# A down projection in groups of two column blocks, some pairs of k-tiles by seven products instead of eight, and a thin gate's weights in one piece

## The chip, the cores and the metric

The kernel runs on one core of one Trainium2 chip. The metric is the device time of one execution in microseconds (us). The engines are called PE (TensorE; PEld is its weight load), DVE (VectorE), ACT (ScalarE), POOL (GpSimd) and SP (SyncE, which here issues the weight loads).

## The reference, cut to what matters

Two blocks are applied to a sequence of 256 tokens of width 2048, all in fp32. The change touches the end of the second block, its gated feed-forward layer, and the very first product of the first block.

```python
# first block: 48 narrow columns of proj (ml_i, ml_f, dn_b, dn_a) are the "thin gate"
u = _rmsnorm(h, norm_w)
proj = jnp.matmul(u, w_in)
...
# second block, FFN_HIDDEN = 5632
h = rmsnorm(x, ffn_norm_w[l])
x = x + (jax.nn.silu(h @ w_gate[l]) * (h @ w_up[l])) @ w_down[l]
return rmsnorm(x, final_norm_w)
```

## The kernel before, in words

**fp32 products from three passes.** Each operand is cut into a high part (cast to fp32r on ACT) and the rest (a subtraction on DVE). A product of two k-tiles is then three matmuls: high by high, high by rest, rest by high. For weights this is `cut`: one ACT cast (L312) and one DVE subtraction (L314) for each piece of 1024 columns, that is two k-tiles of 512. The 256 tokens are two tiles of 128; a normal piece is 12 matmuls of 128x512 (2 k-tiles, 2 token tiles, 3 passes).

**The stream.** All weights are one list of pieces. `run_stream` goes through it: it loads five pieces ahead (SP, tag `wr`, 5 buffers), cuts up to three pieces ahead (tags `wh`, `wl`, 5 buffers each), issues the piece's matmuls, and after each piece lets every side generator go one step (`advance`). What follows a product (evacuation, activation, transposes, the making of the next operand) is such a generator. The order written in the program is a priority: a scheduler at build time orders each engine's queue by it, taking what is ready.

**Seven products instead of eight.** `Pair` computes two 512-column blocks X and Y together. For a pair of k-tiles, two token tiles and two blocks there are eight products of 128x128 by 128x512. For the pairs in `SPAIRS` (1, 3, 5 of 8) it uses Strassen's scheme in Winograd's form: seven products, in four pieces A, E, B, C, whose weights are sums made on DVE (`cut`, L305 to L308, four ops of 128x512), and whose operand forms s1 to s4 are sums of the operand's tiles. The other pairs are two plain pieces X and Y. A sum of products is kept in a PSUM bank of its own: four from the pool `pm` (tag `mm`) and, from the first A on, three from the pool `ps` (tag `sp`). Each pool has four banks, and transposes take theirs from `ps` (`bank`). Before, only the gate and up projections of the feed-forward layer use `Pair`.

**The feed-forward stage.** The hidden width is 11 blocks of 512, in three parts `PARTS` of 4, 4 and 3. For each part, each block is one `Pair` of w_gate and w_up columns (8 pairs of k-tiles; `ff_mid` after the last C, `ff_done` at the end: it evacuates, applies the gate, transposes the block's hidden values on PE (L237) and cuts them into the operand `opf`). Then the part's down projection follows: four chunks of 512 columns n = 0..3, each with 16 k-tiles (12 in the last part) by plain products, with two `pm` banks; `ff_down` adds each to the residual `hw[n]`, scaled by `sc3`. After the last part the final norm is made and written out.

**The start.** `startup` issues the four loads of x and the loads of the first four pieces. The first seven pieces are the thin gate's weights, of 1, 1, 2, 3, 3, 3, 3 k-tiles (`FIRST`), each loaded from two column ranges (32 and 16 columns). Then x is transposed chunk by chunk and turned into the operand (`operand`: an ACT and a DVE op for each of 16 k-tiles, written to `hl`), and `stats` squares x for the norm (ACT, eight ops with a sum).

Of the kernel before, what the change touches and what calls it, by code (L numbers as in the profile page):

```python
# [11 lines left out]
F32 = mybir.dt.float32  # L12
# [7 lines left out]
P = 128  # L20
D = 2048
S = 256
# [11 lines left out]
AHEAD = 5  # L34
SPAIRS = (1, 3, 5)
PARTS = ((0, 4), (4, 8), (8, 11))
WN = 1024
WU = 14
STEP = 2
FIRST = [1, 1, 2, 3, 3, 3, 3]  # L40
MH, DH, AH, GH = 8, 16, 16, 4
# [63 lines left out]
class Pair:  # L105
# [9 lines left out]

    def __init__(self, x, y, nk, opnd, pairs, mid, done):
        self.src, self.nk, self.opnd, self.mid, self.done, self.k0 = {"X": x, "Y": y}, nk, opnd, mid, done, 0
        self.parts = []
        for p in range(nk // 2):
            self.parts += [(2 * p, 2, c) for c in ("AEBC" if p in pairs else "XY")]  # L120
        self.last_s = max(i for i, q in enumerate(self.parts) if q[2] == "C")
        self.po = None
        use = [(i, t[0]) for i, q in enumerate(self.parts) for t in self.PLAN[q[2]]]
        self.first = {b: min(i for i, c in use if c == b) for _, b in use}
        self.final = {b: max(i for i, c in use if c == b) for _, b in use}


# [30 lines left out]
def kernel(ctx, tc, a, out, dbg=None):  # L158
# [115 lines left out]
    def load(i):  # L274
        if i >= len(pieces) or i in raw:
            return
        ch, k, n, part = pieces[i]
        if part in ("B", "C"):
            raw[i] = None
            return  # L280
        w = wp.tile([P, WN], F32, tag="wr", name=nm("wr"), bufs=RB)
        raw[i] = w
        if part is None:
            wv = v3(w[:, :n * ch.width], ch.width)
            c = 0
            for src in ch.src:
                cw_ = src.shape[1]
                SP.dma_start(out=wv[:, :, c:c + cw_],
                             in_=src[(ch.k0 + k) * P:(ch.k0 + k + n) * P, :].rearrange("(k p) n -> p k n", p=P))
                c += cw_  # L290
        else:
            SP.dma_start(out=v3(w, 512), in_=ch.src["X" if part in "XA" else "Y"][k * P:(k + 2) * P, :].rearrange(
                "(k p) n -> p k n", p=P))
# [72 lines left out]
    def run_pair(ch, i, e):  # L366

        _, k0, n, part = pieces[i]
        wh, wl = split.pop(i)
# [114 lines left out]
    def startup():  # L484
# [15 lines left out]
        for _ in range(WU):  # L500
            tr(b[:, :P], ident)
        cut(0)
        cut(1)
        for c in range(4):
            for _ in operand(v3(xin[c], 512), op1, 4 * c, 4, lambda j, c=c: vec(V_NW + 4 * c + j), act1[0], act1[1], 4 * c):
                pass
            if c == 0:
                cut(2)
        sides.append(stats())

    def stats():

# [3 lines left out]
        for c in range(4):  # L516
            for t in range(2):
                act(junk[:, :512], v3(xin[c], 512)[:, t, :], AF.Square, accum_out=ssx[:, t * 4 + c:t * 4 + c + 1])
            yield
# [878 lines left out]
    dform = []  # L1398

    def operand3(nat, n, hi, lo):  # L1400

        f = v3(page(), S)
        for j in (0, 2):
# [12 lines left out]
            p = 2 * n + j // 2  # L1416
            x = half()
            if p in SPAIRS:
                a11, a21, a12, a22 = (f[:, j + q, t * P:(t + 1) * P] for q in range(2) for t in range(2))
                s1, s3, s2, s4 = (x[:, q * P:(q + 1) * P] for q in range(4))  # L1420
                V.tensor_tensor(out=s1, in0=a21, in1=a22, op=ALU.add)
                V.tensor_tensor(out=s3, in0=a21, in1=a11, op=ALU.subtract)
                V.tensor_tensor(out=s2, in0=s1, in1=a11, op=ALU.subtract)
                V.tensor_tensor(out=s4, in0=a12, in1=s2, op=ALU.subtract)
                h, w, c = page(F32R), 512, 0
                names = [(nme, 2 * p) for nme in ("s1", "s3", "s2", "s4")]
            else:
                V.tensor_tensor(out=v3(x[:, :S], P), in0=f[:, j:j + 2, 0:P], in1=f[:, j:j + 2, P:S], op=ALU.subtract)
# [3 lines left out]
                w = S  # L1432
                dform[-1][1] += S
                names = [("d", 2 * p), ("d", 2 * p + 1)]
            A.copy(out=h[:, c:c + w], in_=x[:, :w])
            V.tensor_tensor(out=h[:, 512 + c:512 + c + w], in0=x[:, :w], in1=h[:, c:c + w].bitcast(F32), op=ALU.subtract)
            for q, nme in enumerate(names):
                op3.forms[nme] = (h[:, c + q * P:c + (q + 1) * P], h[:, 512 + c + q * P:512 + c + (q + 1) * P])
            for q in range(2):
# [36 lines left out]
    def ff_done(po, st, part, k0):  # L1476
# [35 lines left out]

    def ff_down(po, n, hf):
# [4 lines left out]
        if hf == len(PARTS) - 1:  # L1518
            jk = half()
            for t in range(2):  # L1520
                act(jk, h[:, t, :], AF.Square, accum_out=ss4[:, t * 4 + n:t * 4 + n + 1])
            fb = half()
            G.dma_start(out=fb, in_=a["final_norm_w_2"].unsqueeze(0)[:, n * 512:(n + 1) * 512].to_broadcast([P, 512]))
            if n < 3:
                yield
                mul(h, h, mid(fb, 2))
                return
            ov = out.rearrange("b (t p) d -> p (b t) d", p=P)
# [101 lines left out]
    for part, (b0, b1) in enumerate(PARTS):  # L1630
        for blk in range(b0, b1):
# [32 lines left out]
```

## Time and profile before

| what | value |
|---|---|
| median of three runs | 2321.31 us (2321.14 to 2323.5) |
| the profiled execution | 2321.42 us |
| its span, first to last instruction | 2319.2 us |
| PE busy | 2303.5 us, 99% |
| DVE busy | 1595.2 us, 69% |
| ACT busy | 1153.0 us, 50% |
| mean granted PE clock | 0.998 |

The profiled execution is 2.2 us longer than its span; what lies around the span is no instruction of the kernel. Busy time of PE is the union of overlapping matmul records, so a single record (some 0.39 us) is longer than the distance to the next one.

### The profile page before, as it was taken

How to read it: one execution, taken by the hardware profiler on the slowest of the kernel's cores; microseconds unless marked ns; L12 is line 12 of the kernel's file. 1: busy time of each engine (PE TensorE's matmuls, PEld its weight loads, DVE VectorE, ACT ScalarE, POOL GpSimd, SP SyncE). 2: the span in 40 equal slices, each digit the busy share in tenths (PEclk: the TensorE clock that was granted, in tenths of full speed). 3: DMA queues.
4: the chain of work that ended last, by engine and by line, in shares of the span. 5: the costliest groups of instructions: out<-in, count | busy, mean ns of one | idle time of the engine just before them, and what ended most of it. 6: DMA issues, size and time to landing. Idle time of an engine off the chain costs nothing.

```text
span 2319.2 us, 29556 instructions
## 1 busy us (share of the span) xinstructions
PE 2303.5 (99%) x11101; PEld 1900.8 (82%) x11101; DVE 1595.2 (69%) x2170; ACT 1153.0 (50%) x1527; POOL 91.3 (4%) x122
## 2 busy tenths in 40 slices
PE   8999999999999999999999999999999999999998
PEld 7888888888888888888888777888888888888887
DVE  6777678785676555455555566667897588856985
ACT  5554445544454444444544456456555355544553
POOL 0102001000100000000010000000000000000000
PEclk9999999999999999999999999999999999999999
DMA  7666545666555666666576554455656556665664
GB/s 238 189 182 205 171 141 168 180 206 182 168 158 164 183 189 193 201 204 203 183 217 181 166 146 142 144 185 163 216 180 227 178 181 204 218 197 175 201 215 138
DMA packets 225390, 427.97 MB, mean 185 GB/s; under 512 B 20392, under 2 KB 20816, under 8 KB 225248
## 3 DMA queue, kind: packets, MB, share of 16 engines
q1 hardware_dynamic: 219328, 411.08, 58.1%
q0 software_dynamic: 5056, 13.70, 2.2%
q8 instruction: 87, 1.43, 0.2%
q10 hardware_dynamic: 864, 1.31, 0.2%
q14 instruction: 55, 0.45, 0.1%
HBM read 422.31 MB, written 3.73 MB: 184 GB/s over the span
## 4 chain that ended last, share of the span: by engine, by line
PE 95%; DMA 2%; DVE 2%; issue 1%; ACT 1%; SPq 0%; POOLq 0%; POOL 0%; DVEq 0%; ACTq 0%
PE mm L219 87%; PE sp L219 4%; PE sp L237 3%; DMA wr<-in_w_up_dram 2%; DVE wl L314 1%; PE sp L795 1%; PE sp L1225 0%; DMA pg<-in_x_dram 0%; ACT wh L312 0%; DVE wr L306 0%; DVE wr L305 0%; ACT pg L216 0%; DVE pg L308 0%; DVE pg L307 0%; DVE pg L1482 0%
## 5 line engine op out<-in xcount | busy, mean ns | idle before, releaser
L219 PE MATMUL mm<-wh,hl 128*128 128x512 f32 x4186 | 1336.9, 393 | 0.1
L314 DVE TENSOR_TENSOR wl<-wr,wh 128x1024 fp32r<-128x1024 f32 (+2 forms) x817 | 967.0, 1193 | 511.3 <-ACT wh L312 508.3
L312 ACT CAST wh<-wr 128x1024 fp32r<-128x1024 f32 (+2 forms) x817 | 830.8, 1026 | 893.8 <-PE mm L219 813.9
L219 PEld LDWEIGHTS mm<-wh,hl 128*128 128x128 f32 x4186 | 783.3, 188 | 166.3 <-issue 4.8
L219 PE MATMUL mm<-wl,hl 128*128 128x512 f32 x2093 | 818.5, 391 | 1.2 <-DVE wl L314 1.1
L219 PE MATMUL mm<-wh,pg 128*128 128x512 f32 x1780 | 565.3, 391 | 0.0
L219 PEld LDWEIGHTS mm<-wl,hl 128*128 128x128 f32 x2093 | 393.3, 188 | 81.3 <-DVE wl L314 2.7
L219 PEld LDWEIGHTS mm<-wh,pg 128*128 128x128 f32 x1780 | 333.7, 188 | 69.9 <-issue 0.9
L219 PE MATMUL mm<-wl,pg 128*128 128x512 f32 x890 | 346.7, 389 | 0.0
L219 PEld LDWEIGHTS mm<-wl,pg 128*128 128x128 f32 x890 | 167.1, 188 | 34.2
L237 PE MATMUL sp<-con,pg 128*128 128x128 f32 x555 | 87.8, 279 | 4.1 <-DMA pg<-in_consts_dram 3.9
L237 PEld LDWEIGHTS sp<-con,pg 128*128 128x128 f32 x555 | 70.0, 144 | 20.0 <-issue 5.6
L312 ACT CAST wh<-pg 128x1024 fp32r<-128x1024 f32 x33 | 34.7, 1052 | 83.1 <-DVE pg L308 55.0
L213 DVE SCALAR_TENSOR_TENSOR pg<-cv,vt,pg 128x255 f32<-128x255 f32 (+2 forms) x144 | 61.6, 479 | 1.3 <-ACT pg L216 1.3
L219 PE MATMUL mm<-wh,cv 128*128 128x512 f32 x176 | 61.5, 390 | 0.0
L314 DVE TENSOR_TENSOR wl<-pg,wh 128x1024 fp32r<-128x1024 f32 x33 | 40.4, 1224 | 23.0 <-ACT wh L312 22.8
L219 PE MATMUL sp<-pg,pg 128*128 128x128 f32 (+3 forms) x320 | 50.3, 315 | 0.0
L219 PEld LDWEIGHTS sp<-pg,pg 128*128 128x128 f32 (+1 forms) x320 | 43.0, 190 | 6.2 <-issue 2.9
L216 ACT ACTIVATE pg<-sp,vt 128x256 fp32r<-128x256 f32 (+1 forms) x64 | 28.3, 470 | 28.4 <-PE sp L237 17.3
L216 ACT ACTIVATE pg<-pg 128x512 f32<-128x512 f32 (+2 forms) x54 | 35.4, 676 | 9.3 <-DMA pg<-in_x_dram 3.2
L219 PEld LDWEIGHTS mm<-wh,cv 128*128 128x128 f32 x176 | 33.0, 188 | 6.7
L305 DVE TENSOR_TENSOR wr<-wr,wr 128x512 f32<-128x512 f32 x33 | 22.8, 691 | 20.8 <-DMA wr<-in_w_up_dram 20.7
(273 smaller groups left out, 1192.1 us busy)
## 6 DMA issues: line engine op xcount, KB each, us to landing
wr<-in_w_in_dram SPq DMA_DIRECT2D x416, 512.0 KB, 3.8
wr<-in_w_out_dram SPq DMA_DIRECT2D x96, 512.0 KB, 4.4
wr<-in_w_gate_dram SPq DMA_DIRECT2D x88, 512.0 KB, 3.8
wr<-in_w_up_dram SPq DMA_DIRECT2D x88, 512.0 KB, 4.6
wr<-in_w_down_dram SPq DMA_DIRECT2D x88, 512.0 KB, 4.4
pg<-zsc POOLq DMA_DIRECT2D x8, 384.0 KB, 4.7
pg<-in_x_dram SPq DMA_DIRECT2D x4, 512.0 KB, 7.3
pg<-gsc POOLq DMA_DIRECT2D x4, 512.0 KB, 6.3
```

The lines of the kernel that those rows point to most:

```text
L213: return V.scalar_tensor_tensor(out=o, in0=x, scalar=s, in1=y, op0=op0, op1=op1)
L216: return A.activation(out=o, in_=x, func=f, **kw)
L219: PE.matmul(o, l, r, start=start, stop=stop)
L237: PE.transpose(o, x, ident[:n, :n])
L305: V.tensor_tensor(out=w3[:, :512], in0=w2[:, :512], in1=w[:, :512], op=ALU.subtract)
L312: A.copy(out=h[:, :sz], in_=x)
L314: V.tensor_tensor(out=l[:, :sz], in0=x, in1=h[:, :sz].bitcast(F32), op=ALU.subtract)
L795: PE.matmul(o, l, r_, start=True, stop=True, tile_position=(row, col))
```

## The change

- The down projection is done in groups of two blocks (n = 0, 1 and n = 2, 3) by a new class `Pair8`. In the first two parts, pairs 2, 4 and 6 of the eight pairs of k-tiles go by seven products. In the last part (six pairs) only the group n = 0, 1 is made so, with pairs 2 and 4; n = 2 and n = 3 stay plain chunks.
- `Pair8` keeps eight sums: four `pm` banks and, from the first A piece on, all four `ps` banks. X and Y need no difference form of the operand.
- The scaling by `sc3` moves from `ff_down` into `ff_done` (two products there get a scalar). For eight blocks (the second to fourth of the first two parts, the second and third of the last) `ff_done` also makes the forms s1 to s4 of the block's first pair of k-tiles (`pair_forms`: a copy and a cast on ACT, five ops on DVE). `down_mid` and `down_pair` add the sums to the residual.
- The thin gate's weights are one piece of 16 k-tiles. In `startup`, the second piece is cut only after the operand is made, and the third is no longer cut there; the squares of `stats` are queued on ACT behind the last operation that makes the operand.

```diff
+DPAIRS = ((2, 4, 6), (2, 4, 6), (2, 4))
-FIRST = [1, 1, 2, 3, 3, 3, 3]
+FIRST = [16]
...
+class Pair8(Pair):
+    PLAN = {**Pair.PLAN, "X": (("2", "a0"), ("4", "a1")), "Y": (("8", "a1"), ("3", "a0"))}
+    BANKS = "2483", "1576"
...
         if ch.po is None:
-            ch.po = {b: pm.tile([P, 512], F32, tag="mm", name=nm("mm")) for b in "2453"}
+            ch.po = {b: pm.tile([P, 512], F32, tag="mm", name=nm("mm")) for b in ch.BANKS[0]}
         if part == "A" and "1" not in ch.po:
-            for b in "176":
+            for b in ch.BANKS[1]:
...
         cut(0)
+        for c in range(4):
+            for ins in operand(v3(xin[c], 512), op1, 4 * c, 4, lambda j, c=c: vec(V_NW + 4 * c + j), act1[0], act1[1], 4 * c):
+                pass
         cut(1)
-        for c in range(4):
-            for _ in operand(v3(xin[c], 512), op1, 4 * c, 4, lambda j, c=c: vec(V_NW + 4 * c + j), act1[0], act1[1], 4 * c):
-                pass
-            if c == 0:
-                cut(2)
-        sides.append(stats())
+        sides.append(stats(ins))
-    def stats():
+    def stats(last):
...
+            with ExitStack() as after:
+                for ins in last:
+                    after.enter_context(tc.issue_after(ins.ins))
+                for t in range(2):
+                    act(junk[:, :512], v3(xin[c], 512)[:, t, :], AF.Square, accum_out=ssx[:, t * 4 + c:t * 4 + c + 1])
...
+    def pair_forms(op, k, f):
+        x = half()
+        a11, a21, a12, a22 = (f[:, q, t * P:(t + 1) * P] for q in range(2) for t in range(2))
+        s1, s3, s2, s4 = (x[:, q * P:(q + 1) * P] for q in range(4))
+        V.tensor_tensor(out=s1, in0=a21, in1=a22, op=ALU.add)
+        V.tensor_tensor(out=s3, in0=a21, in1=a11, op=ALU.subtract)
+        V.tensor_tensor(out=s2, in0=s1, in1=a11, op=ALU.subtract)
+        V.tensor_tensor(out=s4, in0=a12, in1=s2, op=ALU.subtract)
+        h = page(F32R)
+        A.copy(out=h[:, :512], in_=x)
+        V.tensor_tensor(out=h[:, 512:], in0=x, in1=h[:, :512].bitcast(F32), op=ALU.subtract)
...
-        mul(g[:, lo_], g[:, lo_], v[:, hi_])
-        mul(g[:, hi_], g[:, hi_], v[:, lo_])
+        stt(g[:, lo_], g[:, lo_], sc3[:, 0:1], v[:, hi_], ALU.mult, ALU.mult)
+        stt(g[:, hi_], g[:, hi_], sc3[:, 1:2], v[:, lo_], ALU.mult, ALU.mult)
...
+            if (k0 + j) // 2 - 2 * PARTS[part][0] in DPAIRS[part]:
+                f = half()
+                A.copy(out=f, in_=b)
+                pair_forms(opf[part], k0 + j, v3(f, S))
...
+    def down_mid(po, n):
+        h, g = v3(hw[n], 512), v3(hw[n + 1], 512)
+        x, v = page(), page()
+        s1, u, w = x[:, :512], x[:, 512:], v[:, :512]
+        A.copy(out=s1, in_=po["1"])
+        plus(u, s1, po["6"])
+        plus(w, u, po["7"])
+        plus(h[:, 0, :], h[:, 0, :], po["1"])
+        plus(u, u, po["5"])
+        plus(v[:, 512:], w, po["5"])
+        yield
+        plus(g[:, 0, :], g[:, 0, :], u)
+        plus(h[:, 1, :], h[:, 1, :], w)
+        plus(g[:, 1, :], g[:, 1, :], v[:, 512:])
+        yield
+
+    def down_pair(po, n, part):
+        h, g = v3(hw[n], 512), v3(hw[n + 1], 512)
+        for o, b in ((h[:, 0, :], "2"), (h[:, 1, :], "4"), (g[:, 1, :], "8"), (g[:, 0, :], "3")):
+            plus(o, o, po[b])
+        yield
+        if part == len(PARTS) - 1:
+            yield from last_norm(n)
+            yield from last_norm(n + 1)
+
+    def ff_down(po, n, part):
         h = v3(hw[n], 512)
         for t in range(2):
-            stt(h[:, t, :], po[t], sc3[:, t:t + 1], h[:, t, :], ALU.mult, ALU.add)
+            plus(h[:, t, :], h[:, t, :], po[t])
...
-        for n in range(4):
-            add(Chunk([wd[:, n * 512:(n + 1) * 512]], 512, 4 * (b1 - b0), opf[part],
-                      lambda po, n=n, part=part: ff_down(po, n, part), k0=4 * b0))
+        nk, k0 = 4 * (b1 - b0), 4 * b0
+        final = part == len(PARTS) - 1
+        for n in (0,) if final else (0, 2):
+            add(Pair8(wd[:, n * 512:(n + 1) * 512], wd[:, (n + 1) * 512:(n + 2) * 512], nk, opf[part], DPAIRS[part],
+                      lambda po, n=n: down_mid(po, n), lambda po, n=n, part=part: down_pair(po, n, part), k0))
+        for n in (2, 3) if final else ():
+            add(Chunk([wd[:, n * 512:(n + 1) * 512]], 512, nk, opf[part],
+                      lambda po, n=n, part=part: ff_down(po, n, part), k0=k0))
```

`plus` is one DVE addition; `last_norm` is the former end of `ff_down`, unchanged.

## Rows read from the trace of the kernel before

**Rows 1.** The page's first two parts: busy time, and the clock in slices.
```profile
span 2319.2 us, 29556 instructions
PE 2303.5 (99%) x11101; PEld 1900.8 (82%) x11101; DVE 1595.2 (69%) x2170; ACT 1153.0 (50%) x1527; POOL 91.3 (4%) x122
...
PEclk9999999999999999999999999999999999999999
```

**Rows 2.** The page's chain that ended last, shares of the span by engine.
```profile
PE 95%; DMA 2%; DVE 2%; issue 1%; ACT 1%; SPq 0%; POOLq 0%; POOL 0%; DVEq 0%; ACTq 0%
```

**Rows 3.** Stretches: a gate block, and a part's down projection; busy us (instructions).
```profile
core 0: us, PE busy (x) PEld busy (x) DVE busy (x) ACT busy (x) POOL busy (x), PEclk, DMA share, GB/s
1679.70:1722.30 42.60, 42.60 (x192) 35.01 (x192) 38.90 (x47) 24.13 (x27) 0.00 (x0) 1.00 0.61 199
...
1771.50:1851.00 79.50, 79.50 (x356) 65.81 (x355) 44.60 (x43) 31.43 (x32) 0.00 (x0) 1.00 0.60 188
```

**Rows 4.** What PE waited for from 25 to 2310 us: total, times, longest.
```profile
PE mm L219 <- DVE wl L314: 1.1, 3, 0.6
```

**Rows 5.** Timeline of PE in a down projection: start, duration, what.
```profile
1799.81 0.39 PE L219 MATMUL mm<-wh,pg 128*128 128x512 f32 x1
...
1802.75 0.39 PE L219 MATMUL mm<-wl,pg 128*128 128x512 f32 x1
```

**Rows 6.** Groups by line and shape, whole span: busy us, mean ns.
```profile
L314 DVE TENSOR_TENSOR wl<-wr,wh 128x1024 fp32r<-128x1024 f32 x776 | 944.7, 1223 | 505.4 <-ACT wh L312 502.4
L312 ACT CAST wh<-wr 128x1024 fp32r<-128x1024 f32 x776 | 809.8, 1050 | 871.9 <-PE mm L219 792.7 <-issue 54.3 <-DMA wr<-in_w_down_dram 5.4
...
L305 DVE TENSOR_TENSOR wr<-wr,wr 128x512 f32<-128x512 f32 x33 | 22.8, 691 | 20.8 <-DMA wr<-in_w_up_dram 20.7
```

**Rows 7.** Timeline of DVE from a gate block into the down projection.
```profile
1770.66 0.68 DVE L1484 TENSOR_TENSOR pg<-pg,mm 128x512 f32<-128x512 f32 x1
1771.25 1.22 DVE L314 TENSOR_TENSOR wl<-wr,wh 128x1024 fp32r<-128x1024 f32 x1
1772.39 0.68 DVE L1485 TENSOR_TENSOR pg<-pg,mm 128x512 f32<-128x512 f32 x1
1772.99 1.22 DVE L213 SCALAR_TENSOR_TENSOR pg<-pg,pg 128x1024 f32<-128x1024 f32 x1
...
1784.77 0.68 DVE L1504 TENSOR_TENSOR pg<-sp,pg 128x512 fp32r<-128x512 f32 x1
```

**Rows 8.** Timeline of PE there: the last transposes of the gate block.
```profile
1782.34 0.60 PE L237 MATMUL sp<-con,pg 128*128 128x128 f32 x4
```

**Rows 9.** Groups by line and shape from 1500 to 1640 us: one of the forms' sums.
```profile
L1421 DVE TENSOR_TENSOR hp<-pg 128x128 f32<-128x128 f32 x3 | 0.9, 286 | 0.0
```

**Rows 10.** Timeline of SP's queue at the start: DMA issues.
```profile
0.74 0.86 SPq L288 DMA_DIRECT2D wr<-in_w_in_dram  x2
1.65 1.97 SPq L248 DMA_DIRECT2D pg<-in_x_dram  x4
```

**Rows 11.** Groups of ACT by line and shape from 0 to 25 us.
```profile
L216 ACT ACTIVATE hl<-sp,vt 128x256 fp32r<-128x256 f32 x16 | 7.3, 492 | 0.6 <-PE sp L237 0.6
L216 ACT ACTIVATE pg<-pg 128x512 f32<-128x512 f32 x8 | 5.1, 635 | 3.2 <-DMA pg<-in_x_dram 3.2
...
L216 ACT ACTIVATION_READ_ACCUMULATOR pg<-pg 128x1 f32 x8 | 1.6, 199 | 0.0
```

**Rows 12.** Timeline of ACT: the last op that makes the first operand.
```profile
21.50 0.48 ACT L216 ACTIVATE hl<-sp,vt 128x256 fp32r<-128x256 f32 x1
```

**Rows 13.** DMA from 10 to 16 us: packets, bytes, rate, sizes.
```profile
DMA packets 4023, 0.70 MB, mean 117 GB/s; under 512 B 3891, under 2 KB 3891, under 8 KB 4023
```

**Rows 14.** Stretch from 10 to 17 us, columns as in rows 3.
```profile
10.00:17.00 7.00, 5.04 (x30) 4.58 (x29) 5.21 (x16) 7.00 (x25) 0.11 (x1) 0.76 0.65 116
```

**Rows 15.** Timeline of PE and DVE at the end.
```profile
2310.43 0.39 PE L219 MATMUL mm<-wh,pg 128*128 128x512 f32 x1
...
2310.86 0.75 DVE L213 SCALAR_TENSOR_TENSOR pg<-mm,sc,pg 128x512 f32<-128x512 f32 x1 [1.48 <-PE mm L219]
```

More of the change, by code (lines that the diff above doesn't have):

```diff
@@ L114, with __init__ @@
             "C": (("6", "s2", 0), ("4", "a1", 1))}
-    def __init__(self, x, y, nk, opnd, pairs, mid, done):
-        self.src, self.nk, self.opnd, self.mid, self.done, self.k0 = {"X": x, "Y": y}, nk, opnd, mid, done, 0
+    BANKS = "2453", "176"
+    def __init__(self, x, y, nk, opnd, pairs, mid, done, k0=0):
+        self.src, self.nk, self.opnd, self.mid, self.done, self.k0 = {"X": x, "Y": y}, nk, opnd, mid, done, k0
         self.parts = []
@@ L291, in load @@
         else:
-            SP.dma_start(out=v3(w, 512), in_=ch.src["X" if part in "XA" else "Y"][k * P:(k + 2) * P, :].rearrange(
+            SP.dma_start(out=v3(w, 512), in_=ch.src["X" if part in "XA" else "Y"][(ch.k0 + k) * P:(ch.k0 + k + 2) * P, :].rearrange(
                 "(k p) n -> p k n", p=P))
@@ L368, in run_pair @@
         _, k0, n, part = pieces[i]
+        k0 += ch.k0
         wh, wl = split.pop(i)
@@ L516, in stats @@
         for c in range(4):
-            for t in range(2):
-                act(junk[:, :512], v3(xin[c], 512)[:, t, :], AF.Square, accum_out=ssx[:, t * 4 + c:t * 4 + c + 1])
+            with ExitStack() as after:
[3 more added lines that the diff above has]
+                    act(junk[:, :512], v3(xin[c], 512)[:, t, :], AF.Square, accum_out=ssx[:, t * 4 + c:t * 4 + c + 1])
             yield
@@ L1398 @@
     dform = []
+    def pair_forms(op, k, f):
[9 more added lines that the diff above has]
+        V.tensor_tensor(out=h[:, 512:], in0=x, in1=h[:, :512].bitcast(F32), op=ALU.subtract)
+        for q, nme in enumerate(("s1", "s3", "s2", "s4")):
+            op.forms[nme, k] = (h[:, q * P:(q + 1) * P], h[:, 512 + q * P:512 + (q + 1) * P])
     def operand3(nat, n, hi, lo):
@@ L1416, in operand3 @@
             p = 2 * n + j // 2
-            x = half()
             if p in SPAIRS:
[L1419 to L1426, printed above, removed]
+                pair_forms(op3, 2 * p, f[:, j:j + 2, :])
             else:
+                x = half()
                 V.tensor_tensor(out=v3(x[:, :S], P), in0=f[:, j:j + 2, 0:P], in1=f[:, j:j + 2, P:S], op=ALU.subtract)
@@ L1431, in operand3 @@
                 h, c = dform[-1]
-                w = S
                 dform[-1][1] += S
[L1434 to L1438, printed above, removed]
+                A.copy(out=h[:, c:c + S], in_=x[:, :S])
+                V.tensor_tensor(out=h[:, 512 + c:512 + c + S], in0=x[:, :S], in1=h[:, c:c + S].bitcast(F32), op=ALU.subtract)
+                for q in range(2):
+                    w = slice(c + q * P, c + (q + 1) * P)
+                    op3.forms["d", 2 * p + q] = (h[:, w], h[:, 512 + c + q * P:512 + c + (q + 1) * P])
             for q in range(2):
@@ L1511, with plus, last_norm @@
     fin = {}
-    def ff_down(po, n, hf):
+    def plus(o, x, y):
+        V.tensor_tensor(out=o, in0=x, in1=y, op=ALU.add)
+    def down_mid(po, n):
[22 more added lines that the diff above has]
+    def ff_down(po, n, part):
         h = v3(hw[n], 512)
         for t in range(2):
-            stt(h[:, t, :], po[t], sc3[:, t:t + 1], h[:, t, :], ALU.mult, ALU.add)
+            plus(h[:, t, :], h[:, t, :], po[t])
         yield
[L1518 to L1527, printed above, removed]
+        if part == len(PARTS) - 1:
+            yield from last_norm(n)
+    def last_norm(n):
+        h = v3(hw[n], 512)
+        jk = half()
+        for t in range(2):
+            act(jk, h[:, t, :], AF.Square, accum_out=ss4[:, t * 4 + n:t * 4 + n + 1])
+        fb = half()
+        G.dma_start(out=fb, in_=a["final_norm_w_2"].unsqueeze(0)[:, n * 512:(n + 1) * 512].to_broadcast([P, 512]))
+        if n < 3:
+            yield
+            mul(h, h, mid(fb, 2))
+        else:
             ov = out.rearrange("b (t p) d -> p (b t) d", p=P)
```

## The prediction

> **What bounds the kernel now.** First the page's busy times and clock: PE is busy 99% of the span at full clock, DVE 69%, ACT 50% [rows 1]. Busy PE alone proves little, so next the chain that ended last: 95% of it lies on PE, 2% each on DMA and DVE [rows 2]. Then PE's waits: between 25 and 2310 us its matmuls waited 1.1 us, three times, for a weight's rest from DVE [rows 4]. So from 25 us on time goes only with PE instructions, and most of the 2319.2 - 2303.5 = 15.7 us that PE lacks lie at the two ends. The timeline gives the price of one instruction: 13 matmuls start between 1799.81 and 1802.75 us, 2.94 / 13 = 0.226 us each [rows 5]; the 0.39 us of one record overlaps the next and isn't the price.
>
> The stretches show which engine is second. In one gate block's length DVE is busy 38.9 of 42.6 us, 91%, with PE full; in a part's down projection only 44.6 of 79.5, 56% [rows 3]. The change makes the second kind of stretch like the first.
>
> **Matmuls taken away.** A pair of k-tiles for two blocks costs 8 x 3 = 24 matmuls by plain products, 7 x 3 = 21 by seven. The first two parts have two groups with three such pairs each, the last one group with two: 12 + 2 = 14 pairs, 42 matmuls, 42 x 0.226 = 9.5 us. Transposes and bytes loaded stay as they are. The 0.226 us is a row of this very stage. The Trainium skill (TensorE: Matmul & The Clock Gate, Back-to-back issue gap) gives N / 2.4 + 2.5 ns for an isolated warm matmul, 216 ns at 512 columns, and about 131 ns in a sustained stream; by these the term would be 9.1 or 5.5 us. The trace's stream runs at neither, and its row decides.
>
> **DVE's load for it.** Back to back, an op of 128x512 costs 0.60 us and one of 128x1024 1.14 us (the starts at 1770.66, 1771.25, 1772.39 and 1772.99) [rows 7]. The mean durations of 0.69 and 1.22 us overlap likewise [rows 6]. A pair by seven products costs DVE four sums, 2.4 us, and rests of 1024, 512, 1024 and 1024 columns, 3 x 1.14 + 0.60 = 4.0: together 6.4 us, against 21 x 0.226 = 4.7 us of PE. A plain pair costs 2.3 against 5.4. Alone the first is DVE-bound by 1.7 us; with the plain pair after it, 8.7 stands against 10.2.
>
> A group of the new kind has the cuts of a gate block. From its 38.9 us go `ff_mid` (2 ops), `ff_done` (5 sums, 2 products, 2 rests, one op of 1024 columns): 11 x 0.60 + 1.14 = 7.7. Instead come 8 additions of `down_mid` and 4 of `down_pair`: 12 x 0.60 = 7.2. That is 38.4 us in 183 x 0.226 = 41.4, 93%. ACT stays far below: three casts of 1.05 us [rows 6] and a shorter one against 4.7.
>
> The first group of a part is tighter. It still does most of the last gate block's `ff_done`, two sums, the op of 1024 columns, two products and two rests, 6 x 0.60 + 1.14 = 4.7 us, and new forms: four sums of 0.29 us [rows 9] and a rest of 0.69, 1.9 us. Of its own end two ops of `down_pair` and a third of `down_mid`'s, 1.2 + 1.6 = 2.8 us, pass to the next group (my division, from the order in the program). 38.4 + 4.7 + 1.9 - 2.8 = 42.2 stands against 42.6 with its transposes, 99%. The forms also go into five gate blocks: 38.9 + 1.9 = 40.8 of 42.6, 96%. Cuts run up to three pieces ahead, and the group begins with two plain pairs, so I expect small stalls: 0.5 us in each of three first groups, 1.5 in all. The bounds are 0, since stretches at 91% showed nearly none [rows 3, 4], and 5, if each first group once waits out the 1.7 us that a pair lacks. I stay near the lower end, the gate rows being the nearest.
>
> The moved scale costs nothing: the two products become ops of the same size with a scalar. In the plain chunks an addition of 0.68 [rows 7] replaces the 0.75 us op that reads the bank; only the last one lies behind the last matmul [rows 15]: 0.1 us gained.
>
> **The start.** Two things move against each other. Eight squares with their sum reads, 8 x (0.635 + 0.199) = 6.7 us of ACT [rows 11], leave the path of the first operand, whose last ACT op now starts at 21.50 us [rows 12]. But the thin gate's weights are 16 x 128 x 2 = 4096 short runs; between 10 and 16 us 3891 such packets fill the DMA at 117 GB/s [rows 13]. Before, the first piece's two DMAs go ahead of the x loads in SP's queue, though the program issues x first [rows 10]. If the single piece takes that place, 14/16 of these runs move ahead of x: 3584 x 6 / 3891 = 5.5 us later x. The sum is -1.2; I take -1.0. The squares are late instead: they feed `rstd`, first needed by the gates' generator, which PE doesn't wait for, and the evacuation of the first wide block, which lies behind its 96 matmuls, 96 x 0.226 = 22 us of PE, and these cover it. Bounds: PE is idle 2.0 of the 7 us from 10 to 17, at a granted clock of 0.76 (1.7 us more) [rows 14], so at most 3.5 are to be gained. If the piece goes behind x, the weights land as late as now and are cut in one go, some 0.8 us on ACT and 0.9 on DVE, with PE cold: 2 to 3 us lost.
>
> **Sum**, against the profiled 2321.42 us (0.1 above the median of 2321.31): -9.5 + 1.5 - 1.0 - 0.1 gives 2312.3.
>
> **Rivals.**
> *PSUM runs out.* From the third pair on a group holds all eight banks. The last gate block's transposes need two banks of the same pool first; they run at 1782.34 us [rows 8], and their bank is read until 1784.77 + 0.68 = 1785.5 [rows 7]. The gate block's last sum is read at 1772.39 [rows 7], so the third pair, four pieces of 2.7 us later, comes at about 1783, up to 2.5 us before that. For: DVE and ACT will be busier there than in these rows. Against: three banks are free by then, and the fourth is first needed by piece C, 15 matmuls or 3.4 us later. If it waits it costs 1 to 2.5 us in each of three parts, say 5 in place of 1.5: 2315.8. The Trainium skill (Perfetto Trace Analysis, Optimization Strategy) reads the same gap repeating on the engine that should be full as a sign that SBUF or PSUM lacks room for the next tile. No gap of that kind shows before.
>
> *VectorE becomes the bound (slower).* If the cuts' run-ahead doesn't bridge the pairs by seven products, each of the 14 pairs costs its 1.7 us: 24 us, 2334. It decides from 10.6 / 14 = 0.76 us lost for each pair. For: 99% in a first group. Against: gate blocks with the same cuts run at 91% without waits.
>
> *The start gets longer.* The thin piece lands behind x: +2.5 instead of -1.0, 2315.8.
>
> *More than forecast.* No stalls, and the start gains its 3.5: 2308.3.
>
> **Chances.** The forecast (2310 to 2314.5) 0.62; PSUM 0.15; VectorE the bound 0.07; the longer start 0.11; more than forecast 0.05. About 0.2%, 4.6 us, is what a measurement of this kernel can tell from no change; faster means below 2316.7. That holds for the forecast, the larger gain, nearly all of the longer start and half of the PSUM case: 0.84. Within 0.2%: the other half and what little is left of a mild DVE loss, 0.10. Slower: 0.06. The range from 2308.5 to 2317 leaves out the DVE case and the ends of the others.
>
> **What would show it.** The 512-column matmuls fall by 42 at an unchanged 0.226 us; DVE is above 90% in the down projection; PE waits there add up to 1 or 2 us, on the rests of weights. Long waits on transposes or on a third pair's first matmuls mean PSUM. If the thin piece's DMAs go ahead of x and the first operand's last ACT op comes about 1 us before 21.50, the start is as argued; behind x means the third rival. I am wrong if DVE's waits sum to over 5 us, or if the scheduler's new order opens gaps in stages that the change doesn't touch.

## The result and the profile after

The changed kernel takes 2354.34 us (median of four runs, 2353.82 to 2356.01) against 2322.19 for the kernel before in the same rounds: a ratio of 1.0139, 95% interval 1.0126 to 1.0152. It is 32 us slower where 9 us faster was forecast. Since 42 matmuls fewer are worth 9.5 us at the old pitch, about 32.3 + 9.5 = 42 us were lost somewhere.

The page of the changed kernel: busy time, and the busy tenths of PE and DVE in forty slices of the span, to be read against [rows 1]:

```profile
span 2353.0 us, 29655 instructions
PE 2311.0 (98%) x11059; PEld 1892.8 (80%) x11059; DVE 1683.2 (72%) x2328; ACT 1185.6 (50%) x1570; POOL 91.4 (4%) x122
...
PE   8999999999999999999999999999999899989998
...
DVE  6777677785666655455555566668888888888986
```

The count of matmuls fell by 42, as it should, but PE's busy time rose by 7.5 us, and what PE lacks of the span went from 15.7 to 2353.0 - 2311.0 = 42.0 us. So 26.3 us are new idle time, and 7.5 + 9.5 = 17.0 us are matmul records that became longer or overlap less. The mean granted clock is 0.995, against 0.998 before; on 2353.0 and 2319.2 us that is about 11.8 - 4.6 = 7 us of the 17. The rest of the 17 I put down, without a view that shows it, to the end of the last record ahead of each wait, which overlaps nothing. DVE took 88.0 us more.

The chain that ended last, shares by engine, against [rows 2], and PE's waits from 25 to 2330 us, against [rows 4]:

```profile
PE 85%; DVE 7%; DMA 5%; issue 2%; ACT 1%; SPq 0%; DVEq 0%; POOLq 0%; POOL 0%; ACTq 0%
```

```profile
engine line waited for: us in total, times, longest us
PE mm L230 <- DVE wl L325: 11.2, 10, 2.8
PE mm L230 <- ACT wh L323: 8.5, 10, 2.8
PE mm L230 <- DVE pg L1539: 5.0, 6, 2.2
PE mm L230 <- DVE pg L1502: 1.3, 2, 0.8
PE mm L230 <- DVE pg L1505: 0.2, 1, 0.2
```

PE waits for the rests of weights (L325), their casts (L323), and for banks that the sums at a group's end have not emptied (L1539 in `down_mid` and `down_pair`, L1502 and L1505 in `ff_done`). The five rows add up to 26.2 us, as much as the new idle time. No transpose is in the list. Stretches of the changed kernel show where: the third pair of the first group, then the five ends of groups, two in each of the first two parts and one in the last (columns as in [rows 3]).

```profile
1786.00:1796.00 10.00, 8.50 (x42) 6.74 (x41) 8.19 (x11) 4.60 (x7) 0.00 (x0) 1.00 0.46 148
1814.00:1842.00 28.00, 23.15 (x93) 17.99 (x92) 24.80 (x33) 11.62 (x13) 0.00 (x0) 0.94 0.50 163
1863.00:1890.00 27.00, 23.28 (x91) 17.66 (x91) 24.19 (x31) 10.99 (x12) 0.00 (x0) 0.94 0.54 172
...
2088.00:2112.00 24.00, 19.54 (x76) 14.76 (x75) 21.15 (x28) 8.17 (x9) 0.00 (x0) 0.93 0.54 177
2138.00:2162.00 24.00, 20.70 (x80) 15.56 (x79) 21.70 (x29) 9.23 (x10) 0.00 (x0) 0.93 0.50 155
...
2303.00:2322.00 19.00, 16.82 (x75) 13.61 (x74) 17.33 (x21) 9.36 (x15) 0.93 (x2) 1.00 0.76 252
```

At 0.226 us each, 93 matmuls are 21.0 us of the 28 at the first end of a group: 7.0 lost. In the same way the other four lose 6.4, 6.8, 5.9 and 2.1 us, 28 in all. At the third pair (the first line, whose 42 records hold short transposes too) PE waits once for 1.5 us, and in the other two first groups for 1.5 and 1.2: 4 us. The remaining 10 us have no stretch of their own here. Gate blocks that also make forms are one place for them; a run below looks at these alone.

The timeline of DVE at the first of these ends, and PE's there:

```profile
1819.39 1.28 DVE L1539 TENSOR_TENSOR pg<-pg,mm 128x512 f32<-128x512 f32 x2
1820.58 2.35 DVE L325 TENSOR_TENSOR wl<-wr,wh 128x1024 fp32r<-128x1024 f32 x2
1822.85 1.28 DVE L1539 TENSOR_TENSOR pg<-pg,mm 128x512 f32<-128x512 f32 x2
1824.05 0.69 DVE L1539 TENSOR_TENSOR pg<-pg,pg 128x512 f32<-128x512 f32 x1
1824.65 0.69 DVE L316 TENSOR_TENSOR wr<-wr,wr 128x512 f32<-128x512 f32 x1
1825.25 0.69 DVE L317 TENSOR_TENSOR wr<-wr 128x512 f32<-128x512 f32 x1
1825.85 1.22 DVE L325 TENSOR_TENSOR wl<-wr,wh 128x1024 fp32r<-128x1024 f32 x1
1826.99 1.29 DVE L1539 TENSOR_TENSOR pg<-pg,pg 128x512 f32<-128x512 f32 x2
```

```profile
1823.66 0.61 PE L230 MATMUL mm<-wh,pg 128*128 128x512 f32 x2
1827.13 0.50 PE L230 MATMUL mm<-wl,pg 128*128 128x512 f32 x1 [2.85 <-DVE wl L325]
...
1829.52 0.63 PE L230 MATMUL mm<-wl,pg 128*128 128x512 f32 x1
1829.95 1.05 PE L230 MATMUL mm<-wh,pg 128*128 128x512 f32 x2
1830.80 0.63 PE L230 MATMUL mm<-wl,pg 128*128 128x512 f32 x1
```

DVE never stops here. The rest for which PE waits starts at 1825.85; the additions of `down_mid` and two weight sums stand ahead of it in the queue. After the wait PE runs four matmuls, waits 0.61 us more for a bank (L1539), and then the pitch is 0.43 us (1829.52 to 1829.95, two more to 1830.80) in place of 0.226.

Three queues feed one another: SP issues a load only when DVE has read a raw buffer, and ACT's casts and DVE's weight sums wait for loads. What SP waited for from 1780 to 1885 us in the changed kernel, and then in the groups with plain pairs only (the second run below), where nothing is lost:

```profile
SPq L303 <- DVE wl L325: 74.1, 27, 10.0
```

```profile
SPq L303 <- DVE wl L325: 88.3, 38, 9.0
```

So SP's waiting alone is no sign of a loss: it is longer where PE waits for nothing. What differs is what stands behind the loads. ACT's casts from 1600 to 2330 us, in the changed kernel and in the plain groups:

```profile
ACT wh L323 <- DMA wr<-in_w_down_dram: 22.2, 23, 3.0
```

```profile
ACT wh L323 <- DMA wr<-in_w_down_dram: 8.0, 6, 2.8
```

DVE's weight sums from 1776 to 1885 us in the changed kernel (in the plain groups it waited 4.6 us for loads there), and the rate of the loads in 40 slices of one microsecond from 1800 us:

```profile
DVE wr L316 <- DMA wr<-in_w_down_dram: 7.9, 5, 2.0
```

```profile
GB/s 279 283 283 49 242 252 10 55 283 201 209 236 111 150 297 375 324 291 285 287 322 250 35 236 266 346 178 2 0 0 0 0 92 309 346 270 31 0 0 0
```

From 1823 to 1830 DVE gets through one cut, at 1825.85, so hardly a buffer comes free, and the loads stop (0 GB/s from 1828 to 1832). At 1836.80 DVE then has waited 0.96 us for a load that came late. At the third pair it waited 1.75 us for one:

```profile
1786.83 1.22 DVE L325 TENSOR_TENSOR wl<-pg,wh 128x1024 fp32r<-128x1024 f32 x1
1789.81 0.69 DVE L316 TENSOR_TENSOR wr<-wr,wr 128x512 f32<-128x512 f32 x1 [1.75 <-DMA wr<-in_w_down_dram]
```

A pair by seven products holds three of the five raw buffers (X, Y and a buffer of its weight sums, `w3` in `cut`), which leaves two to load ahead.

### The profile page after: what moved, and what is told of

Same layout as the page of the kernel before. It is cut to its first block, busy times and chain, and to the rows that moved or that the text cites. A ratio compares the mean times of both kernels' runs of the same rounds, so it can differ in the third digit from the quotient of the medians.

```text
span 2353.0 us, 29655 instructions
## 1 busy us (share of the span) xinstructions
PE 2311.0 (98%) x11059; PEld 1892.8 (80%) x11059; DVE 1683.2 (72%) x2328; ACT 1185.6 (50%) x1570; POOL 91.4 (4%) x122
## 4 chain that ended last, share of the span: by engine, by line
PE 85%; DVE 7%; DMA 5%; issue 2%; ACT 1%; SPq 0%; DVEq 0%; POOLq 0%; POOL 0%; ACTq 0%
PE mm L230 77%; PE sp L230 4%; DVE wl L325 3%; DMA wr<-in_w_down_dram 3%; PE sp L248 2%; DMA wr<-in_w_up_dram 1%; DVE pg L1539 1%; ACT wh L323 1%; PE sp L809 1%; DVE wr L317 1%; PE sp L1239 0%; DVE pg L318 0%; DVE wr L316 0%; DVE pg L319 0%; DMA wr<-in_w_in_dram 0%
## 5 line engine op out<-in xcount | busy, mean ns | idle before, releaser
L325 DVE TENSOR_TENSOR wl<-wr,wh 128x1024 fp32r<-128x1024 f32 (+2 forms) x825 | 973.2, 1191 | 439.0 <-ACT wh L323 435.9
L323 ACT CAST wh<-wr 128x1024 fp32r<-128x1024 f32 (+2 forms) x825 | 838.4, 1026 | 829.0 <-PE mm L230 723.8
L323 ACT CAST wh<-pg 128x1024 fp32r<-128x1024 f32 x47 | 49.5, 1052 | 91.5 <-DVE pg L319 46.6
L325 DVE TENSOR_TENSOR wl<-pg,wh 128x1024 fp32r<-128x1024 f32 x47 | 57.6, 1225 | 29.6 <-ACT wh L323 29.4
L316 DVE TENSOR_TENSOR wr<-wr,wr 128x512 f32<-128x512 f32 x47 | 32.5, 692 | 37.9 <-DMA wr<-in_w_down_dram 19.1
```

Source lines behind the costliest of these rows:

```text
L316: V.tensor_tensor(out=w3[:, :512], in0=w2[:, :512], in1=w[:, :512], op=ALU.subtract)
L323: A.copy(out=h[:, :sz], in_=x)
L325: V.tensor_tensor(out=l[:, :sz], in0=x, in1=h[:, :sz].bitcast(F32), op=ALU.subtract)
```

## The experiments

Four theories stood against each other. *The load*: DVE's added work itself isn't hidden, wherever it stands. *The burst*: it would be, if the sums at a group's end didn't come all at once. *The order*: DVE's queue puts weight sums that wait for a load ahead of the sums that free banks. *The banks*: eight sums and the transposes don't fit into PSUM. Where an expectation gives theories numbers, what it expects of each says which is meant. All ratios are to the kernel before, with its 95% interval.

**The start alone.** The kernel before, with the new start.
```diff
-FIRST = [1, 1, 2, 3, 3, 3, 3]
+FIRST = [16]
```


> The kernel before with the change's start alone: the thin gate's weights in one piece, the second piece cut after the operand, the squares queued behind it. If the start costs what the marker of the feed-forward stage shows (its first Tanh at 1606.7 us after against 1605.9 before), about 1 us more than before, 2322 to 2324 us. If the start's new order had disturbed later stages, some of the 32 us would be here: 2330 or more.


2322.37 us, ratio 0.9997 [0.9988, 1.0007]: no gain and no loss that can be told from noise.

**Groups with plain pairs only.** The changed kernel with no pair by seven products and no forms.
```diff
-DPAIRS = ((2, 4, 6), (2, 4, 6), (2, 4))
+DPAIRS = ((), (), ())
```


> The changed kernel with no pair by seven products in the down projection: groups of two blocks with four PSUM banks, no operand forms, no sums of weights, no second set of banks. Theory 1 (the 32 us come from VectorE's work for the pairs by seven products, its amount or its place): no stalls, 2321 to 2325 us. Theory 2 (the change-over between groups stalls, because a group takes all four banks of its pool and the next must wait until they are read): the five change-overs go on costing some 6 us each, 2345 to 2352 us.


2320.84 us, 0.9994 [0.9984, 1.0003], and PE waits for nothing from 25 us on. Grouping two blocks, the moved scale and a group's first four banks cost nothing that can be told from noise. The cost lies in what this run leaves out: the products by seven with their sums, forms and second set of banks.

**Another order of pairs.** The products earlier in a group, so that two plain pairs stand behind the last of them.
```diff
-        for p in range(nk // 2):
+        for p in order or range(nk // 2):
...
+                      (0, 1, 2, 4, 3, 5) if final else (0, 2, 1, 4, 3, 6, 5, 7) if n else (0, 1, 2, 3, 4, 6, 5, 7)))
```


> The changed kernel with the same pairs by seven products, but the pairs of a group taken in another order, so that two plain pairs stand at its end, as in a gate block (0 1 2 3 4 6 5 7 in a part's first group, 0 2 1 4 3 6 5 7 in the second, 0 1 2 4 3 5 in the last part). VectorE's work is the same. Theory 1a (the place: the eight sums that follow the last C, the four that free the banks and the cuts crowd into the one plain pair before the change-over): most of the 29 us at the change-overs go, 2325 to 2335 us. Theory 1b (the amount of VectorE's work in a group is too much wherever it stands): no change or worse, 2350 to 2360 us.


2344.37 us, 1.0099 [1.0082, 1.0115]: 9 us back, at the same DVE work. That lies between the two expectations: the place is a part of the cause, not most of it.

**`down_mid` later.**
```diff
     s1, u, w = x[:, :512], x[:, 512:], v[:, :512]
+    yield from wait(3)
```


> The changed kernel with the eight sums behind the last C issued three steps later, that is behind the four sums that free the banks of the next group. Theory 1a in the form that VectorE's order is at fault (sums that nobody waits for stand ahead of the cuts and of the sums that free banks): the change-overs shrink by half or more, 2325 to 2340 us. Theory 1b: no change, 2350 to 2360 us. If the next block then waits for the second set of banks, a new wait shows at its first seven-product pair, and the time is 2350 or more for that reason.


2344.71 us, 1.0097 [1.0078, 1.0116], again between the two. The burst is part of it, 10 of 42 us.

**Forms that nobody reads.** The plain groups, with the forms of the same eight blocks made.
```diff
-DPAIRS = ((2, 4, 6), (2, 4, 6), (2, 4))
+DPAIRS = ((), (), ())
...
-            if (k0 + j) // 2 - 2 * PARTS[part][0] in DPAIRS[part]:
+            if (k0 + j) // 2 - 2 * PARTS[part][0] in ((2, 4, 6), (2, 4, 6), (2, 4))[part]:
```


> As e2 (groups of two blocks, all pairs plain), but the hidden block's operand forms s1 to s4 are made all the same, and nobody reads them: two ACT ops and five DVE ops for eight blocks. If the gate blocks with forms, at some 96% of VectorE, stall by themselves: 2 to 4 us for each of the three parts, 2327 to 2332 us. If they only matter together with the groups: as e2, 2320 to 2323 us.


2328.99 us, 1.0023 [1.0014, 1.0033]. So 11.5 us of DVE work (1604.6 busy, against 1593.1 without) cost 5 to 7 us, in gate blocks whose own products are as before. The forms' ACT work, 8.2 us, is in this too. Where two blocks meet, DVE waits for the load of a weight sum, for longer than the 0.91 us of the plain groups at the same place:
```profile
1726.91 0.69 DVE L316 TENSOR_TENSOR wr<-wr,wr 128x512 f32<-128x512 f32 x1 [1.37 <-DMA wr<-in_w_up_dram]
```

**Two pairs in a group.**
```diff
+DPAIRS = ((2, 5), (2, 5), (2,))
```


> The changed kernel with two pairs by seven products in a group (2 and 5 of eight, 2 of six in the last part) in place of three (two in the last): 27 matmuls fewer than before instead of 42 (6.1 us), VectorE's work in a group about 34 of 42 us, and two plain pairs behind the last C. If VectorE's amount and place are the whole cause: nearly no stalls, 2315 to 2320 us. If any group with sums behind it stalls at the change-over: 2330 us or more.


2331.78 us, 1.0034 [1.0021, 1.0047], as expected if any group with sums behind it stalls. Its DVE has this at a group's end, with two bank-freeing sums queued behind weight sums that wait for a load:
```profile
1814.08 0.69 DVE L316 TENSOR_TENSOR wr<-wr,wr 128x512 f32<-128x512 f32 x1 [1.32 <-DMA wr<-in_w_down_dram]
1814.69 0.68 DVE L317 TENSOR_TENSOR wr<-wr 128x512 f32<-128x512 f32 x1
1815.29 1.22 DVE L325 TENSOR_TENSOR wl<-wr,wh 128x1024 fp32r<-128x1024 f32 x1
1816.42 1.28 DVE L1539 TENSOR_TENSOR pg<-pg,mm 128x512 f32<-128x512 f32 x2
```
That picture gave rise to the theory of the order, which the ninth to twelfth runs try.

**Sums on GpSimd.** The fourth run, with the sums that read no PSUM (15 of `down_mid`, 32 of the forms) on GpSimd.
```diff
-    plus(g[:, 0, :], g[:, 0, :], u)
+    plus(g[:, 0, :], g[:, 0, :], u, G)
```


> As e4 (the eight sums three steps later), with the sums that touch no PSUM moved from VectorE to GpSimd: three of the eight sums, and the four small sums of each operand form; 5 x 1.8 + 8 x 0.8 us, some 15 us of VectorE's work. Theory amount: time falls by about as much as that work, 2330 us. If GpSimd is slow or gets in VectorE's way at the memory: 2345 us or more.


2348.48 us, 1.0104 [1.0087, 1.0121], no gain over the fourth run, as expected of a GpSimd that is slow or in the way. 19 us of DVE work left (9.8 and 9.2 by the groups of lines), but DVE's busy time fell by only 5.9, to 1676.3.

**A sixth raw buffer**, in place of a page.
```diff
-RB = 5
+RB = 6
...
-PGB = 23
+PGB = 22
```


> The changed kernel with six instead of five buffers for loaded weights (and 22 instead of 23 pages to make room). VectorE waited four times for weights in the first groups, because a load is issued only when a buffer has been read. If these waits are the cause: 2335 to 2345 us. If VectorE's work or order is: unchanged within 5 us of 2354.


2347.26 us, 1.0101 [1.0086, 1.0116]: 8.8 us back by the ratios, between the two expectations. Late loads are a part of the cause.

**The order, three times.** Weight sums are queued behind the sums that free banks, and the cut of an A piece of the next pair of blocks is begun a step later: on the fourth run, on the sixth, and on the fifth.
```diff
+            with ExitStack() as after:
+                for ins in freed:
+                    after.enter_context(tc.issue_after(ins.ins))
                 V.tensor_tensor(out=w3[:, :512], in0=w2[:, :512], in1=w[:, :512], op=ALU.subtract)
...
             for j in range(CUT):
+                if i + j < len(pieces) and pieces[i + j][3] == "A" and pieces[i + j][0] is not ch:
+                    break
                 cut(i + j)
```


> As e4 (three pairs by seven products, the eight sums three steps later), with VectorE's queue ordered: the sums of weights for the next block's or group's first seven-product pair are queued behind the sums that free the block's PSUM banks. Theory 3 (the loss is an order in VectorE's queue: sums of weights that wait for their load stand ahead of the sums that free banks): most of the remaining 22 us go, 2315 to 2325 us. Theory 1b (amount): as e4, 2340 us or more.

> As e6 (two pairs by seven products), with the queue ordered as in e9. Theory 3: the waits at the change-overs and in the gate blocks with forms go, 2315 to 2319 us, 6 us below the kernel before. Theory 1b: as e6, 2329 to 2333 us.

> As e5 (groups plain, operand forms made and not used), with the queue ordered as in e9. Theory 3: the 6 us that the forms cost in e5 go, 2320 to 2324 us. If the forms' VectorE time itself is the cost: as e5, 2327 to 2331 us.


2354.83, 2343.24 and 2352.85 us; 1.0139, 1.0086 and 1.0129, against 1.0097, 1.0034 and 1.0023 without it. All three are worse, by 10, 12 and 25 us: PE now waits for weights, 12.0 us on DVE (L329, the rest) in the last of them. Waits for banks are nearly gone in them, and weights are late instead. But these runs change two things. A cut that begins a step later also keeps raw buffers longer: from 1600 to 2330 us DVE waits 35.9 us for loads of w_up in the last of them, against 20.3 in the fifth run. So they show that this other order is worse, and not that the order in DVE's queue costs nothing.

**The order in the kernel before.** The edit makes the sums of `ff_done` that free banks queue behind the next pair's first two weight sums.


> The kernel before with one change: the sums that free a gate block's PSUM banks are queued on VectorE behind the first two sums of weights of the next block's first seven-product pair. No work is added. Theory 3: each of the eight changes from gate block to gate block within a part stalls PE by 1 to 3 us, 2330 to 2345 us. If that order is harmless: 2320 to 2324 us.


2322.05 us, 0.9998 [0.9989, 1.0008]. The edit changed next to nothing: its trace has the forced order, but the kernel before has it already, at all eight changes from gate block to gate block. The second weight sum and the first sum that frees a bank, in this run and then in the kernel before:
```profile
1639.96 0.68 DVE L307 TENSOR_TENSOR wr<-wr 128x512 f32<-128x512 f32 x1
...
1641.17 0.68 DVE L1485 TENSOR_TENSOR pg<-pg,mm 128x512 f32<-128x512 f32 x1
```
```profile
1638.54 0.68 DVE L306 TENSOR_TENSOR wr<-wr 128x512 f32<-128x512 f32 x1
...
1639.74 0.68 DVE L1481 TENSOR_TENSOR pg<-pg,mm 128x512 f32<-128x512 f32 x1
```
So this run is no test of its own. What the kernel before shows is that the order alone doesn't stall PE in gate blocks without forms. Whether it costs something in the changed kernel, on top of the added work, no run tells.

**Work left out, part by part.** The changed kernel without the four weight sums of its 14 pairs (B and C take the plain weights); without the eight additions and the copy of `down_mid`; without the forms (a plain tile stands for each); and without the last two together.
```diff
+        if part == "A" and isinstance(ch, Pair8):
+            raw[i + 2], raw[i + 3] = w, raw[i + 1]
...
-lambda po, n=n: down_mid(po, n)
+lambda po, n=n: None
...
-                pair_forms(opf[part], k0 + j, v3(f, S))
+                for nme in ("s1", "s3", "s2", "s4"): opf[part].forms[nme, k0 + j] = (v3(hi, S)[:, j, :P], v3(lo, S)[:, j, :P])
```


> The changed kernel without the four sums of weights of each down pair by seven products (14 x 2.4 us of VectorE's work; the pieces B and C take plain weights instead, so the sums of products are not the reference's; the matmuls are as many). Theory 1b (VectorE's amount of work decides): the pairs no longer lack time, and the 42 us fall to about 15, 2325 to 2332 us. If only the work at the end of a group and the forms count: 2345 us or more.

> The changed kernel without the eight sums and the copy behind a group's last C (5 x 5 us of VectorE's work; their four sums of products are left out of the output). Theory 1a (the crowding before the change-over): some 25 to 30 us of the 42 go, 2323 to 2332 us. Theory 1b: about half of that, 2335 to 2342 us.

> The changed kernel without the operand forms (the products that need s1 to s4 take a plain tile of the operand instead, so the output is not the reference's): 8 x 1.9 us less on VectorE, 8 x 1.1 on ACT. e5 priced the forms at 6 us with nobody to read them; if that holds here too, 2345 to 2349 us. If they also set off the waits in the first groups: 2335 to 2342 us.

> e14 and e15 together: only the cuts and sums of weights are left of the added VectorE work, and the four sums that free banks. If cuts and sums of weights fit beside 21 matmuls as they do in gate blocks, this shows the whole gain of 42 matmuls: 2311 to 2316 us. If not, what stays above 2312 is their price.


2334.38, 2338.64, 2340.27 and 2322.56 us; 1.0050 [1.0035, 1.0065], 1.0067 [1.0050, 1.0084], 1.0078 [1.0062, 1.0093] and 0.9999 [0.9990, 1.0009]. The first lies between its two expectations, the second where the amount of work decides, the third where the forms also set off waits in the first groups, and the fourth far from the whole gain. Each part gives time back, none all of it, and the last two add up (16.7 + 14.2 us alone, 32.5 together). With the 20.7 us of the weight sums that is more than the 41.8 lost, so the parts don't act independently. The run without weight sums also needs one raw buffer less for each pair (`w3`), so its 20.7 us aren't DVE's work alone. ACT isn't behind these gains: its busy time is 1185.6 us in the changed kernel, and 1185.2 and 1183.7 in the first two of these runs. With both `down_mid` and the forms gone, the cuts and weight sums still eat the 9.5 us of matmuls. PE waits for rests only:
```profile
PE mm L230 <- DVE wl L325: 7.6, 8, 2.4
```

**Products where DVE has most room.** The second groups of the first two parts alone, with three pairs (1, 3, 5) or two (1, 3); blocks 0 and 1 and the last part are plain chunks; the forms are a side generator of block 0.
```diff
+    def late_forms(part):
+        for k, hi, lo in late[part]:
+            f = half()
+            V.tensor_tensor(out=f, in0=hi.bitcast(F32), in1=lo.bitcast(F32), op=ALU.add)
+            pair_forms(opf[part], k, v3(f, S))
+            yield
```


> The changed kernel with products only in the group of output blocks 2 and 3 of the first two parts (pairs 1, 3 and 5); blocks 0 and 1 of every part and all of the last part are plain chunks, and the forms are made while block 0 and 1 of the part run, from the operand's own two tiles. 18 matmuls less than before (18 x 0.226 = 4.1 us). If what counts is only how crowded VectorE is where the work stands: 2318 to 2321 us, faster than before, with no wait of TensorE for the forms. If any such burst stalls TensorE at the end of the group (about 3 us at each of two places, as with two pairs in e6): 2322 to 2326 us, the same or slower.

> As e17, with two pairs (1 and 3) in each of the two groups: 12 matmuls less (2.7 us), and four plain pairs behind the last product. If crowding decides: 2319.5 to 2321.5 us, with at most 1 us of waits at the two ends of groups. If each burst stalls TensorE: 2322 to 2325 us.


2328.47 us, 1.0028 [1.0019, 1.0037], and 2324.06 us, 1.0006 [0.9997, 1.0015]. The first is slower, and slower than either expectation; the second is not to be told from before, as expected if each burst stalls. The forms did not go where I put them: the build-time scheduler took them up into the gate blocks as soon as their tiles were there. In the trace of the first:
```profile
1712.03 0.68 DVE L1538 TENSOR_TENSOR hp<-pg,pg 128x512 f32<-128x512 f32 x1
...
1713.23 0.28 DVE L1419 TENSOR_TENSOR hp<-hp 128x128 f32<-128x128 f32 x1
```
So the gate blocks' waits of the fifth run are there again (PE waits 5.6 us for L1502, four times). Whether the products pay with forms truly made late was not tried.

## Why the prediction was wrong

**All versions on one scale.** The time lost is the ratio's excess over one, times 2322, plus 0.226 us for each matmul saved (counts from the pages); a ratio's interval moves it by 2 to 4 us either way. DVE's added work is its busy time less the 1593.1 us of the plain groups.

| version | matmuls saved | DVE added, us | time lost, us |
|---|---|---|---|
| changed kernel | 42 | 90.1 | 41.8 |
| sixth raw buffer | 42 | 89.7 | 33.0 |
| `down_mid` later | 42 | 89.1 | 32.0 |
| other order of pairs | 42 | 88.8 | 32.5 |
| no forms | 42 | 78.1 | 27.6 |
| no `down_mid` sums | 42 | 66.4 | 25.1 |
| two pairs a group | 27 | 65.1 | 14.0 |
| no weight sums | 42 | 56.5 | 21.1 |
| neither `down_mid` nor forms | 42 | 54.2 | 9.3 |
| second groups, three pairs | 18 | 45.5 | 10.6 |
| second groups, two pairs | 12 | 33.5 | 4.1 |
| forms unread | 0 | 11.5 | 5.3 |
| sums on GpSimd | 42 | 83.2 | 33.6 |
| ordered, `down_mid` later | 42 | 87.8 | 41.8 |
| ordered, two pairs a group | 27 | 63.9 | 26.1 |
| ordered, forms unread | 0 | 10.4 | 30.0 |

The matmuls saved are worth 9.5 / 90.1 = 0.105 us for each microsecond that the change puts on DVE; the loss is 41.8 / 90.1 = 0.46. The smallest loss is 4.1 / 33.5 = 0.12, where 2.7 / 33.5 = 0.08 was saved; by its interval it lies between 0.06 and 0.19, so that version is at break-even, as is the one with neither `down_mid` nor forms. Placement and buffers move the loss at the same work (33 instead of 42), but not to zero. Nor is the amount of work a price by itself: with the cuts a step later, 10.4 us of it cost 30.0.

**Matmuls.** Right: 42 fewer. In stretches without waits the pitch stays as in [rows 5].

**DVE's load.** Right in size. The prediction's terms give 14 x (2.4 + 1.7) for the pairs, 5 x 4.8 for the ends of groups and 8 x 1.9 for the forms, 96.6 us; 88.0 were measured. The share came out below its 99%, for example 24.80 of 28 us at the end of the first group, because the waits stretched the time.

**The stalls: the step that failed.** "Cuts run up to three pieces ahead ... so I expect small stalls: 0.5 us in each of three first groups, 1.5 in all", with an upper bound of 5. In the place of this term the runs show a loss of about 42 us. The term put nothing at the second groups (93%), and their ends in the first two parts lost 6.4 and 5.9 us; it put nothing at gate blocks with forms (96%), and these alone cost 5. Two things were wrong in it. The bound took a sum over a whole group for what decides, though at a group's end some seven microseconds of additions come between cuts that are needed at once. And the run-ahead is no constant: it hangs on raw buffers that DVE frees, so a late DVE makes late loads (none for four microseconds from 1828 on), and DVE waits for a late load in order, with its other work behind it. A sixth buffer gave 8.8 of the 42 us back; that much at least hangs on the buffers. The gate blocks at 91% [rows 3, 4] were taken as proof of room to 99%; the run with unread forms shows that 11.5 us more in them already cost 5.

**The rivals.** *VectorE becomes the bound* is what happened, with 3 us per pair rather than 1.7 (41.8 / 14), and its place wasn't the pair but mostly the end of a group: 28 of 42 us. The argument against it, that gate blocks at 91% run without waits, fell. *PSUM runs out* didn't happen as described: PE never waited for a transpose's bank, and the wait at the third pair is for a rest, behind a late load. Waits for banks of sums are 6.5 of the 26.2 us, and each of them ends with a DVE addition that empties the bank. The rule quoted there from the Trainium skill (Perfetto Trace Analysis, Optimization Strategy), a repeating gap as a possible sign that SBUF or PSUM lacks room, did in part point the right way, to SBUF: one more raw buffer gave 8.8 us back, and 33.0 stayed lost.

**The start.** Its 1.0 us gained didn't show: the effect is not to be told from zero (the first run's interval is -2.8 to +1.6 us). The thin piece did go ahead of x, and from 10 to 17 us the clock is 1.00 instead of 0.76 [rows 14], but ACT's last two operations that make the operand start at 22.84 us, not a microsecond before 21.50 [rows 12]. (The bound on the gain was added up wrongly, too: 2.0 + 1.7 is 3.7 us, not 3.5.)
```profile
0.74 1.93 SPq L299 DMA_DIRECT2D wr<-in_w_in_dram  x2
2.72 2.06 SPq L259 DMA_DIRECT2D pg<-in_x_dram  x1
```
```profile
22.84 0.87 ACT L227 ACTIVATE hl<-sp,vt 128x256 fp32r<-128x256 f32 x2 [0.54 <-DVE hl L224]
```

**The gaps in untouched stages**, named as a danger, are there in part, in gate blocks whose own products the change leaves alone: they come with the forms, and the plain groups have none.

**Left open.** How the loss divides at the ends of groups between DVE's plain excess, the order in its queue and the loop through late loads isn't settled: a sixth buffer and a later `down_mid` gave 9 to 10 us each and weren't tried together, and no run changed the order alone. Why the late cuts cost 25 us with unread forms and only 10 to 12 in the other two is open. No version beat the kernel before.

## What to carry to other kernels

Price a cut in the bound engine's work by what it adds to the engine behind it: here 0.105 us saved stood against 0.46 lost for each microsecond put on a VectorE that was then about 90% busy, and the mildest versions only broke even. Look at the busiest ten microseconds and at the buffers that its progress frees, not at the share of a whole stage; in an in-order queue with loads that wait for buffers, lateness can come back as more lateness. Before a run that forces an order, look whether the trace has that order already. Test the added work of the second engine by itself first, its results unread, before building what needs it.

## What was not expected of the hardware

- At four of the five ends of groups the granted clock fell to its lower level, 1.2 of 2.4 GHz. At the first it is 0.50 from 1829 to 1832 us, with seven matmuls in 3.00 us; ahead of that PE had waited 2.85 us, run four matmuls 0.23 to 0.34 us apart, and waited 0.61 us more. So the stalls cost more than their own length.
```profile
1829.00:1832.00 3.00, 3.00 (x7) 2.42 (x8) 2.88 (x5) 0.10 (x1) 0.00 (x0) 0.50 0.00 0
```
Not every wait is followed by this. The clock stayed at 1.00 after 2.19 us at the fifth end, and after 2.36 us in the run with neither `down_mid` nor forms. With two pairs in a group, after a wait of 1.69 us, the pitch was full again within one matmul:
```profile
1817.25 0.47 PE L230 MATMUL mm<-wh,pg 128*128 128x512 f32 x1 [1.69 <-DVE pg L1539]
1817.55 0.39 PE L230 MATMUL mm<-wl,pg 128*128 128x512 f32 x1
1817.78 0.63 PE L230 MATMUL mm<-wh,pg 128*128 128x512 f32 x2
```
- An addition of 128x512 takes 1609 ns on GpSimd (whose spans the profile has only roughly) against 685 on VectorE, and with GpSimd at work VectorE's own sums lengthen. One of the weight sums, in the run with `down_mid` later and then in the run with GpSimd:
```profile
L317 DVE TENSOR_TENSOR wr<-wr 128x512 f32<-128x512 f32 x47 | 32.2, 684 | 0.0
```
```profile
L317 DVE TENSOR_TENSOR wr<-wr 128x512 f32<-128x512 f32 x47 | 36.5, 777 | 0.0
```
The Trainium skill (Perfetto Trace Analysis, Optimizing Scalar/DVE Operations) says that the two engines share a read port of SBUF, so that moving work between them might not help; the trace agrees, with 19 us moved and 5.9 gained on VectorE; the weight sums and rests that stayed there take some 10 us more in the groups of lines.
